# A two-layer hybrid decoder trunk on one core: expert rows scaled after turning, pass 0 by one-hot products, choice by differences

## The chip, the cores and the metric

One core of a Trainium2 chip runs the whole kernel; the other cores are idle. The metric is the device time of one execution in microseconds. The kernel was run three times for its time, and once more under the profiler.

## The reference, cut to what matters

Two decoder layers over 512 tokens of width 1024, in float32. Each layer has three kinds of attention, one output projection, a layer norm, a mixture of 16 experts of which every token takes two, and a second layer norm. What the change touches is the stretch from the first norm to the experts:

```python
x = layer_norm(DEEPNORM_ALPHA * x + einsum('bsm,md->bsd', mix, w_out[l]), ln1_g[l], ln1_b[l])
scores = sigmoid(dot(x, w_router))
biased = (scores + router_bias).reshape(N, N_GROUPS, EXPERTS_PER_GROUP)
g_sel = argmax(sum(top_k(biased, 2)[0], axis=-1))       # one group of four experts for a token
_, local = top_k(biased[g_sel], 2)                      # two experts of that group
w = scores[expert] / sum(scores[expert])
h = silu(x @ w_gate[e]) * (x @ w_up[e]) * gate          # for the tokens of expert e
y = h @ w_down[e]
x = layer_norm(DEEPNORM_ALPHA * x + y, ln2_g[l], ln2_b[l])
```

## The kernel before, in words

**Order of the work.** The program is written as many small streams (Python generators). A planner, the class Flow (line 97), plays them against a simple model of the engines with a cost for each step, always takes the step that can start first (its start plus 0.002 us times the stream's priority number decides, so that a low number wins a tie), and emits its instructions at once. Each engine executes its own queue strictly in the order emitted; the waits between engines come from the data. The costs are the writer's: `pe(0.22, f)` books 0.22 us of TensorE.

**Layout.** Tokens lie in 4 blocks of 128 (NT), the width in 8 slices of 128 (KD). `X[:, t]` holds block t, token per partition. The 8 PSUM banks are split into two pools, ACC and PS, of four banks each in the stretch in question.

**From the projection to the choice.** `s_wout` (917) makes the output projection, its second half block by block; `s_half` (968) adds the residual and takes statistics of each half-row; `s_stat` (975) gives mean and inverse deviation, the last step on POOL. `s_router` (1022) does not wait for the norm: it turns the raw rows, multiplies them with `wg` (router weights times the norm's scale) and corrects for mean, deviation and shift afterwards on VectorE (1041, 1045, 1046). `s_norm1` (1055) uses `s_norm` (982): four VectorE steps of half a row per block (990, 998) write the normed rows into X, and a DMA on SP's queue (1060) copies them to `XD` in HBM. `s_choose` (1064), for two blocks at a time, computes the scores from exp (1070) and then the rank of each expert in its group from two comparisons, is_ge and is_gt, that are combined (1084 to 1088), the best group by a maximum (1092 to 1096), the one-hot `ohb` of the chosen experts (1098), the one-hot of each of the two choices `oh` (1104) and the end of the chosen expert's table (`eb`, 1106, 1107).

**From the choice to the rows.** Each expert has 96 slots (CAP), and 16x96 slots make 12 passes (NP) of 128 slots. `s_rank` (1177) counts on TensorE how many earlier tokens chose the same expert (1188 to 1191), picks each choice's position with `oh` (1195, 1198), moves a position beyond the end far away (1200, 1201) and splits it into pass and slot (1203 to 1212). `s_table` (1228) turns that into the list of token numbers by slot with 16 small products (1221, 1225). `s_gather` (1451) fetches for each pass the 128 rows of its slots from XD by an indirect DMA from POOL (1293) into one of three buffers. `turn_rows` (1484) turns them on TensorE (1503) and `s_rows` (1462) evacuates them, half a pass on ScalarE and half on VectorE (279, 280).

**The passes.** `s_passes` (1576) runs, for p = 0 to 11, the first products of pass p (1594: gate and up, 32 columns of slots per expert unit), the turns for pass p-1's hidden rows (1500) and for pass p+1's rows (1503), and the second products of pass p-1 (`second`, 1557, product at 1568). Pass 0 has no second products behind it. `s_act` (1468) takes silu on ScalarE and the product with it on VectorE (1472, 1473). Expert weights are loaded by `s_load_experts` (1346) on SP's queue into buffers as these come free. While TensorE has nothing to do between the projection and pass 0, `s_warm` (1117) books dummy products of ones (1124) until the first gather is due.

**After the passes.** `s_alpha` (1615) multiplies blocks 0 and 2 of X with the residual's factor on POOL or ScalarE; blocks 1 and 3 get it through a product with `ident_alpha` (1673). `s_combine` (1650) adds the experts' results. `overflow` (1369) handles experts with more than 96 tokens, behind a branch.

Of the kernel before, what the change touches and what calls it, by code (L numbers as in the profile page):

```python
# [6 lines left out]
F32 = mybir.dt.float32  # L7
# [27 lines left out]
FAR = 8192.0  # L35

# [159 lines left out]
def body(tc, sb, pp, dr, x, w_in, attn_sinks, c_q_norm_g, c_kv_norm_g, w_uq, w_ukv, w_out, ln1_g, ln1_b,  # L196
# [105 lines left out]
    ident_alpha = fixed(P)  # L302
    V.tensor_scalar(ident_alpha, ident, ALPHA, None, op0=OP.mult)
# [16 lines left out]
    desc = fixed(4)  # L320
    V.tensor_scalar(desc, iotf[:, :4], -1.0, float(NE), op0=OP.mult, op1=OP.add)
    lower = fixed(4, 4)
    G.iota(lower, pattern=[[1, 4], [-1, 4]], base=0, channel_multiplier=0, allow_small_or_imprecise_dtypes=True)
    V.tensor_scalar(lower, lower, 0.0, None, op0=OP.is_gt)
# [45 lines left out]
    for key, n in (("sg", 2 * NE), ("zz", 2 * NE), ("bi", 2 * NE), ("c1", 8 * NE), ("c2", 8 * NE), ("g4", 2 * NE), ("rk", 2 * NE), ("gs", 8), ("m1", 8),  # L370
                   ("pick", 8), ("oh", 4 * NE), ("wts", 4), ("posk", 4), ("row", 4), ("eb", 4), ("op", 4 * NP)):
        for q in range(NT // 2):
            small((key, q), n)
# [105 lines left out]
    def layer(l, xready, prev_free):  # L479
# [542 lines left out]
        def s_router(t):  # L1022
            yield E("gain")
            r0, z = smalls["r0", t], smalls["zz", t // 2][:, t % 2 * NE:(t % 2 + 1) * NE]
            for h in range(2):
# [17 lines left out]
            yield E("stat", t)  # L1043
            mv, rs = smalls["mv", t], smalls["rs", t]
            yield ve(16, lambda: V.scalar_tensor_tensor(r0, gbv[:, 0], mv[:, 0:1], r0, op0=OP.mult, op1=OP.subtract))
            e = yield ve(16, lambda: V.scalar_tensor_tensor(z, r0, rs[:, 0:1], gbv[:, 1], op0=OP.mult, op1=OP.subtract))
# [8 lines left out]
        def s_norm1(t):  # L1055
            yield E("gb1")
# [4 lines left out]
            flow.set(E("xd", t), xd)  # L1061


        def s_choose(q):
# [5 lines left out]
            t = yield ac(32, lambda: A.activation(sg, smalls["zz", q], AF.Exp), [flow.now])  # L1070
            flow.set(E("exp", q), t)
            C1, C2 = (c.rearrange("p (g a b) -> p g a b", a=4, b=4) for c in (c1, c2))
            b84, G84, R84 = (a.rearrange("p (g a) -> p g a", a=4) for a in (bi, g4, rk))
            other = b84[:, :, None, :].to_broadcast([P, 8, 4, 4])
            own = b84[:, :, :, None].to_broadcast([P, 8, 4, 4])
            gs2, pick2 = (a.rearrange("p (t g) -> p t g", t=2) for a in (gs, pick))
# [5 lines left out]
            e = yield v(lambda: V.tensor_tensor(bi2, sg2, rb[:, None, :].to_broadcast([P, 2, NE]), op=OP.add))  # L1082

            yield v(lambda: V.tensor_tensor(C1, other, own, op=OP.is_ge))
            yield v(lambda: V.tensor_tensor(C2, other, own, op=OP.is_gt), [e])
            yield v(lambda: V.tensor_tensor(C1, C1, lower[:, None, :, :].to_broadcast([P, 8, 4, 4]), op=OP.mult), [])
            yield v(lambda: V.tensor_tensor(C1, C1, C2, op=OP.max))
            yield v(lambda: V.tensor_reduce(R84, C1, axis=AX.X, op=OP.add))
# [3 lines left out]
            yield v(lambda: V.tensor_reduce(m1[:, 0:2], gs2, axis=AX.X, op=OP.max))  # L1092
            yield v(lambda: V.tensor_tensor(pick2, gs2, m1[:, 0:2, None].to_broadcast([P, 2, 4]), op=OP.is_equal))
            yield v(lambda: V.tensor_tensor(pick2, pick2, desc[:, None, :].to_broadcast([P, 2, 4]), op=OP.mult))
# [682 lines left out]
```

## Time and profile before

| what | us |
|---|---|
| median of three runs (861.07, 863.41, 863.6) | 863.41 |
| the profiled execution | 862.1 |
| its span, first to last instruction | 860.3 |
| TensorE busy in it (96%) | 821.7 |
| VectorE busy (59%) | 509.6 |
| ScalarE busy (37%) | 315.3 |

The page gives busy times of PE (TensorE), PEld (its weight loads), DVE (VectorE), ACT (ScalarE) and POOL (GpSimd), and then the groups of instructions that cost most. A timeline lists an engine's instructions in order of time: start, duration, line and operation, tiles written and read, how many alike follow one another, and in brackets how long the engine was idle before and what ended the idle time. TensorE's instructions overlap, so a duration is longer than the distance to the next start. PE busy includes the dummy products.

### The profile page before, as it was taken

Reading aid. Unit: us, or ns where it says so; the run is one execution under the profiler, and the core shown is the slowest. Engines: PE = TensorE matmul, PEld = TensorE weight load, DVE = VectorE, ACT = ScalarE, POOL = GpSimd, SP = SyncE. Lnnn points to the kernel's source line nnn. Section 1 sums busy time; section 2 is a strip of 40 time slices with the busy share of each in tenths; the row PEclk is TensorE's granted clock in tenths of the full one; section 3 lists DMA queues with packets and bytes.
Section 4 is the critical chain, followed back from the end, with each engine's and each line's share of the span. In section 5 each row is a group of like instructions: output and inputs, shape, how many; then the busy total and the mean of one; then the engine's idle time right before and its main releaser. Section 6 shows DMA issues by size and latency. Waiting matters only on the chain. (4 is left out here: it accounts for less than half of the span.)

```text
span 860.3 us, 16084 instructions
## 1 busy us (share of the span) xinstructions
PE 821.7 (96%) x6288; PEld 536.8 (62%) x6288; DVE 509.6 (59%) x1504; ACT 315.3 (37%) x790; POOL 103.8 (12%) x135
## 2 busy tenths in 40 slices
PE   7999999999999999979999999999999999999795
PEld 7878886668894333323587889766788743334232
DVE  6799999955681120002998999999458413100057
ACT  4434647963111222212145274677521012221111
POOL 1010102000111111100211001300100111110004
PEclk9999999999999999989999999999999999999898
DMA  8422430175377999976544217010946489999562
GB/s 267 142 77 86 137 134 26 28 266 181 121 252 242 350 370 376 371 266 246 182 102 141 74 50 269 2 50 29 339 147 219 146 306 371 372 372 369 192 265 98
DMA packets 119148, 172.82 MB, mean 201 GB/s; under 512 B 12102, under 2 KB 95558, under 8 KB 119057
## 3 DMA queue, kind: packets, MB, share of 16 engines
q1 hardware_dynamic: 112720, 156.12, 52.8%
q0 software_dynamic: 6336, 15.52, 5.0%
q8 instruction: 53, 0.87, 0.4%
q14 instruction: 39, 0.31, 0.1%
HBM read 154.01 MB, written 25.17 MB: 208 GB/s over the span
## 5 line engine op out<-in xcount | busy, mean ns | idle before, releaser
L283 PE MATMUL bank<-ring,ra 128*128 128x512 f32 (+4 forms) x448 | 167.1, 373 | 0.5 <-ACT fa L605 0.5
L1594 PE MATMUL bank<-fa,ra 128*32 128x512 f32 x1080 | 161.3, 599 | 1.2 <-DVE ra L280 0.7
L284 PE MATMUL bank<-ring,xl 128*128 128x512 f32 (+4 forms) x448 | 157.6, 352 | 0.9 <-DVE xl L452 0.9
L285 PE MATMUL bank<-ring,ra 128*128 128x512 f32 (+4 forms) x448 | 157.9, 353 | 0.0
L279 ACT ACTIVATE fa<-bank 128x512 f32<-128x512 f32 (+3 forms) x170 | 85.4, 516 | 155.9 <-PE bank L441 82.7
L1473 DVE TENSOR_TENSOR fa<-fa,bank 128x256 f32<-128x256 f32 x24 | 10.1, 419 | 214.6 <-ACT fa L1472 214.6
L1594 PEld LDWEIGHTS bank<-fa,ra 128*32 128x32 f32 x1080 | 50.3, 111 | 75.0 <-issue 67.6
L1568 PE MATMUL bank<-fa 128*32 128x512 f32 x504 | 83.8, 625 | 11.1 <-PEq L1376 10.0
L283 PEld LDWEIGHTS bank<-ring,ra 128*128 128x128 f32 x448 | 85.0, 190 | 14.9 <-issue 7.1
L285 PEld LDWEIGHTS bank<-ring,ra 128*128 128x128 f32 x448 | 84.8, 189 | 8.2
L284 PEld LDWEIGHTS bank<-ring,xl 128*128 128x128 f32 x448 | 85.2, 190 | 7.4 <-DVE xl L452 1.3
L441 PE MATMUL bank<-fa 128*128 128x128 f32 (+1 forms) x456 | 71.6, 281 | 7.3 <-DMA fa<-in_x_dram 5.5
L441 PEld LDWEIGHTS bank<-fa 128*128 128x128 f32 (+1 forms) x456 | 55.3, 144 | 24.1 <-issue 6.0
L474 ACT ACTIVATE ring<-fa 128x1024 fp32r<-128x1024 f32 (+4 forms) x56 | 49.4, 897 | 55.7 <-PE bank L284 52.4
L1594 PE MATMUL bank<-ring,ra 128*32 128x512 f32 x360 | 67.1, 592 | 0.0
L1472 ACT ACTIVATE fa<-bank 128x256 f32<-128x256 f32 x24 | 9.2, 384 | 153.0 <-PE bank L1594 153.0
L475 DVE TENSOR_TENSOR ring<-fa,ring 128x1024 fp32r<-128x1024 f32 (+4 forms) x56 | 57.9, 1041 | 7.5 <-ACT ring L474 7.4
L747 DVE MATCH_REPLACE8 aux<-fa,aux 128x256 f32<-128x256 f32 (+2 forms) x96 | 51.6, 540 | 0.0
L746 DVE MAX8 fa<-aux 128x8 f32<-128x256 f32 (+2 forms) x96 | 50.3, 547 | 0.1
L1568 PEld LDWEIGHTS bank<-fa 128*32 128x32 f32 x504 | 19.6, 112 | 46.7 <-issue 44.9
L787 PE MATMUL bank<-fa 64*128 64x256 f32 (+7 forms) x256 | 47.4, 413 | 0.0
L800 ACT ACTIVATE fa<-fa 128x256 f32<-128x256 f32 (+3 forms) x89 | 44.5, 503 | 0.0
(222 smaller groups left out, 1219.3 us busy)
## 6 DMA issues: line engine op xcount, KB each, us to landing
fa<-in_w_gate_dram SPq DMA_DIRECT2D x45, 512.0 KB, 9.4
fa<-in_w_up_dram SPq DMA_DIRECT2D x45, 512.0 KB, 10.4
fa<-in_w_down_dram SPq DMA_DIRECT2D x21, 1024.0 KB, 9.7
xl<-in_w_down_dram SPq DMA_DIRECT2D x9, 1024.0 KB, 11.6
fa<-in_w_out_dram SPq DMA_DIRECT2D x8, 1024.0 KB, 5.9
yd<-fa SPq DMA_DIRECT2D x16, 512.0 KB, 8.3
ring<-in_w_gate_dram SPq DMA_DIRECT2D x15, 512.0 KB, 9.0
ring<-in_w_up_dram SPq DMA_DIRECT2D x15, 512.0 KB, 8.9
```

The source lines that it names most:

```text
L279: return Step([("A", 0.05 + n / 1200, lambda: A.activation(dst, src, AF.Copy)), ("V", 0.12 + n / 960, lambda: V.tensor_copy(dst, src))], a ...
L283: T.matmul(ps, xh, wh, start=start, stop=False)
L284: T.matmul(ps, xl, wh, start=False, stop=False)
L285: T.matmul(ps, xh, wl, start=False, stop=stop)
L441: T.transpose(ps[:n, j, :], s, ident)
L474: yield Step([("A", 0.09 + n / 1200, lambda: A.activation(hv, raw, AF.Copy))], None)
L475: t = yield ve(n, lambda: V.tensor_tensor(lv, raw, hv.bitcast(F32), op=OP.subtract))
L746: yield ve(nk, lambda: V.max(m8, sc))
L747: yield ve(nk, lambda: V.match_replace(sc, m8, sc, MARK))
L787: T.matmul(got[1][:, a * nk:(a + 1) * nk], qs[h], ks[h], start=True, stop=True)
L1568: T.matmul(a[1][cs], ht[:, j, cs], E("raw", e, 2).got[1][:, j, n * 512:(n + 1) * 512], start=j == 0, stop=j == 1)
L1594: T.matmul(acc[1][cs], gh[:, 4 * u + j, cs], E("raw", e, u).got[1][:, j], start=u + j == 0, stop=u + j == 4)
```

## The change

In words: the first norm's scale and shift are no longer applied before the rows are written to HBM. `s_norm1` makes (x - mean) / deviation in one ScalarE step per block, and that is written and gathered; scale and shift come in when a pass's turned rows are evacuated, where they are a number per partition, so that each of the 8 slices has its own instruction. X itself gets scale, shift and the residual's factor in a new `s_alpha` on VectorE, four half-row steps for every block, once pass 0's rows and the table are made and the row is written. Pass 0's rows are not gathered any more: `s_first` builds, for each block, the matrix m of zeros and ones that says which token stands in which of slots 0 to 127, and multiplies X's block with it on TensorE, accumulated over the four blocks into two banks, which gives the rows turned. The choice ranks by one subtraction and one comparison with a tiny negative threshold below the diagonal instead of two comparisons combined, for experts and groups alike, and the limit of an expert's table is applied to all positions before a choice's own is picked.

```diff
 def s_router(t):
     ...
-    e = yield ve(16, lambda: V.tensor_tensor(r0, r0, gp[1][:, :NE], op=OP.add))
+    tp = e
+    es = yield E("stat", t)
+    mv, rs = smalls["mv", t], smalls["rs", t]
+    e = yield ve(16, lambda: V.scalar_tensor_tensor(r0, gbv[:, 0], mv[:, 0:1], r0, op0=OP.mult, op1=OP.subtract), [es])
+    e = yield ve(16, lambda: V.scalar_tensor_tensor(r0, r0, rs[:, 0:1], gbv[:, 1], op0=OP.mult, op1=OP.subtract), [e])
+    e = yield ve(16, lambda: V.scalar_tensor_tensor(z, gp[1][:, :NE], rs[:, 0:1], r0, op0=OP.mult, op1=OP.subtract), [e, tp])
 def s_norm1(t):
-    e = yield from s_norm(t, (aux.of(F32), gb1), E("stat", t).got, er, None, True)
+    for h in range(2):
+        yield E("seen", h, t)
+    e = yield ve(1, lambda: V.tensor_scalar(rs[:, 1:2], mv[:, 0:1], rs[:, 0:1], -1.0, op0=OP.mult, op1=OP.mult), [er])
+    e = yield ac(D, lambda: A.activation(X[:, t], X[:, t], AF.Identity, scale=rs[:, 0:1], bias=rs[:, 1:2]), [e])
+def s_alpha(t):
+    yield E("gb1")
+    yield E("first")
+    yield E("table")
+    yield E("xd", t)
+    for h in range(2):
+        yield ve(512, lambda: V.scalar_tensor_tensor(X[:, t, cs], X[:, t, cs], ALPHA, g[:, cs], op0=OP.mult, op1=OP.mult))
+        e = yield ve(512, lambda: V.scalar_tensor_tensor(X[:, t, cs], b[:, cs], ALPHA, X[:, t, cs], op0=OP.mult, op1=OP.add))
 def s_choose(q):
+    def beaten(c, vals, n, left):
+        yield v(lambda: V.tensor_tensor(c, vals[:, :, None, :].to_broadcast([P, n, 4, 4]), vals[:, :, :, None].to_broadcast([P, n, 4, 4]),
+                                        op=OP.subtract))
+        yield v(lambda: V.tensor_tensor(c, c, beats[:, None].to_broadcast([P, n, 4, 4]), op=OP.is_gt))
+        yield v(lambda: V.tensor_reduce(left, c, axis=AX.X, op=OP.add))
     ...
+    yield from beaten(C1, b84, 8, R84)
     ...
+    yield from beaten(C2, gs2, 2, pick.rearrange("p (t g) -> p t g", t=2))
+    yield v(lambda: V.scalar_tensor_tensor(G84, pick[:, :, None].to_broadcast([P, 8, 4]), 8.0, R84, op0=OP.mult, op1=OP.add))
+    e = yield v(lambda: V.tensor_scalar(ohb[:, 2 * q:2 * q + 2].rearrange("p t e -> p (t e)"), g4, 2.0, None, op0=OP.is_lt))
     ...
+    e = yield v(lambda: V.tensor_tensor(oh.rearrange("p (k e) -> p k e", k=2), g4[:, None, :].to_broadcast([P, 2, 2 * NE]),
+                                        iotf[:, :2, None].to_broadcast([P, 2, 2 * NE]), op=OP.is_equal))
 def s_warm():
-    while E("gathered").t is None or flow.free["T"] < E("gathered").t:
+    while E("warm").t is None or flow.free["T"] < E("warm").t:
+def s_first():
+    for t in range(NT):
+        yield E("posk", t // 2)
+        yield E("normed", t)
+        ...
+        yield v_small(lambda: V.tensor_scalar(m[:, t], iotf, pos[0], None, op0=OP.is_equal), [])
+        te = yield v_small(lambda: V.scalar_tensor_tensor(m[:, t], iotf, pos[1], m[:, t], op0=OP.is_equal, op1=OP.add))
+        if t == NT - 1:
+            flow.set(E("warm"), te)
+        def f():
+            for k in range(KD):
+                T.matmul(banks_[k // 4][1][:, k % 4 * P:(k % 4 + 1) * P], X[:, t, k * P:(k + 1) * P], m[:, t], start=t == 0 and k % 4 == 0,
+                         stop=t == NT - 1 and k % 4 == 3)
+        te = yield pe(0.109 * KD, f, [te])
+flow.go(B0 + 62.9, s_first())
 def s_rows(p, banks_, te):
-    for h in range(2):
-        t = yield from turned(banks_[h], banks_[h][1].rearrange("p (a b) -> p a b", b=P), te, E("gt", p).got[0][:, 4 * h:4 * h + 4])
+    for k in range(KD):
+        dst, src = E("gt", p).got[0][:, k], banks_[k // 4][1][:, k % 4 * P:(k % 4 + 1) * P]
+        g, b = gcol[:, 0, k:k + 1], gcol[:, 1, k:k + 1]
+        t = yield Step([("A", 0.22, lambda: A.activation(dst, src, AF.Identity, scale=g, bias=b)),
+                        ("V", 0.21, lambda: V.tensor_scalar(dst, src, g, b, op0=OP.mult, op1=OP.add))], [te])
 def s_passes():
-    yield from turn_rows(None, 0, GT)
+    te = yield E("first")
+    ...
+    flow.go(B0 + PRIO["experts"] - 20, s_rows(0, E("first").got, te))
-for p in range(NP):
+for p in range(1, NP):
     flow.go(B0 + PRIO["experts"], s_gather(p))
```

The old `s_alpha` on POOL or ScalarE goes, as does `ident_alpha`: the product at 1673 takes the plain identity. `s_rank` compares the positions with the limits right after the rank products, before it needs the one-hots of the choices. The overflow branch gets the same scale and shift.

## Rows read from the trace of the kernel before

**Rows 1.** The page: its first line and the busy times of the engines.

```profile
span 860.3 us, 16084 instructions
...
PE 821.7 (96%) x6288; PEld 536.8 (62%) x6288; DVE 509.6 (59%) x1504; ACT 315.3 (37%) x790; POOL 103.8 (12%) x135
```

**Rows 2.** Busy time by stretch: PE, PEld, DVE, ACT, POOL, then PE clock, DMA share, GB/s.

```profile
239.40:260.90 21.50, 20.44 (x351) 19.71 (x350) 15.16 (x84) 2.96 (x6) 3.79 (x4) 1.00 0.68 236
...
660.20:681.90 21.70, 20.38 (x351) 19.64 (x349) 15.16 (x83) 2.95 (x6) 3.66 (x4) 1.00 0.66 229
```

**Rows 3.** Timeline of PE, first layer: start us, us, engine, line, operation, tiles.

```profile
239.38 1.74 PE L1124 MATMUL bank<-ones 128*128 128x128 bf16 x28
240.96 0.61 PE L441 MATMUL bank<-fa 128*128 128x128 f32 x4
...
242.31 1.06 PE L1035 MATMUL bank<-fa 128*128 128x16 f32 x8 [0.17 <-ACT fa L279]
...
250.17 0.17 PE L1191 MATMUL bank<-ohb,before 128*128 128x16 bf16 x1 [0.25 <-DVE ohb L1098]
...
253.22 0.69 PE L1221 MATMUL bank<-rv,sl 128*128 128x24 bf16 x16
...
259.56 1.10 PE L1503 MATMUL bank<-fa 128*128 128x128 f32 x8 [0.39 <-DMA fa<-xd,ti]
260.90 7.16 PE L1594 MATMUL bank<-fa,ra 128*32 128x512 f32 x64 [0.25 <-ACT ra L279]
267.99 1.09 PE L1503 MATMUL bank<-fa 128*128 128x128 f32 x8
```

**Rows 4.** Timeline of DVE in the same stretch.

```profile
241.24 0.14 DVE L1098 SCALAR_TENSOR_TENSOR ohb<-fa 128x32 bf16<-128x32 f32 x1
...
243.41 0.17 DVE L1041 TENSOR_TENSOR fa<-fa,bank 128x16 f32<-128x16 f32 x1 [0.53 <-PE bank L1035]
...
244.44 0.23 DVE L1046 SCALAR_TENSOR_TENSOR fa<-fa 128x16 f32<-128x16 f32 x1
...
244.72 0.74 DVE L998 SCALAR_TENSOR_TENSOR fa<-fa 128x512 f32<-128x512 f32 x1
245.38 0.17 DVE L1080 TENSOR_SCALAR fa<-fa 128x32 f32<-128x32 f32 x1
...
246.20 0.28 DVE L1084 TENSOR_TENSOR fa<-fa 128x128 f32<-128x128 f32 x1
...
249.94 0.18 DVE L1098 SCALAR_TENSOR_TENSOR ohb<-fa 128x32 bf16<-128x32 f32 x1
...
250.75 0.21 DVE L1195 TENSOR_TENSOR fa<-fa,bank 128x64 f32<-128x64 f32 x1
250.99 0.22 DVE L1198 TENSOR_REDUCE fa<-fa 128x4 f32<-128x64 f32 x1
...
251.44 0.16 DVE L1201 SCALAR_TENSOR_TENSOR fa<-fa 128x4 f32<-128x4 f32 x1
...
253.95 0.18 DVE L1225 TENSOR_SCALAR ti<-bank 128x24 int32<-128x24 f32 x1 [0.41 <-PE bank L1221]
```

**Rows 5.** Timeline of ACT in the same stretch.

```profile
244.70 0.23 ACT L1070 ACTIVATE fa<-fa 128x32 f32<-128x32 f32 x1 [2.45 <-DVE fa L1046]
...
268.16 0.38 ACT L1472 ACTIVATE fa<-bank 128x256 f32<-128x256 f32 x1 [6.36 <-PE bank L1594]
```

**Rows 6.** Timeline of POOL in the same stretch.

```profile
255.02 1.26 POOL L1293 DMA_INDIRECT fa<-xd,ti  x1 [12.88 <-DVE fa L1144]
...
257.89 0.99 POOL L1293 DMA_INDIRECT fa<-xd,ti  x1 [0.31 <-issue]
```

**Rows 7.** The page's costliest groups: busy us, mean ns, idle before and its releaser.

```profile
L1594 PE MATMUL bank<-fa,ra 128*32 128x512 f32 x1080 | 161.3, 599 | 1.2 <-DVE ra L280 0.7
```

**Rows 8.** Timeline of SP's queue, first layer.

```profile
264.60 0.37 SPq L1355 DMA_DIRECT2D fa<-in_w_gate_dram  x1
```

**Rows 9.** Busy time by stretch, columns as in group 2, middle of the experts' stage.

```profile
300.00:320.00 20.00, 20.00 (x184) 7.83 (x188) 6.55 (x16) 6.11 (x11) 4.04 (x4) 1.00 1.07 372
```

More of the change, by code (lines that the diff above doesn't have):

```diff
@@ L35 @@
 FAR = 8192.0
+TINY = 1.5e-38
+NONE = 4096.0
 class Event:
@@ L1069, in s_choose @@
             sg2, bi2 = (a.rearrange("p (t e) -> p t e", t=2) for a in (sg, bi))
-            t = yield ac(32, lambda: A.activation(sg, smalls["zz", q], AF.Exp), [flow.now])
+            t = yield ac(32, lambda: A.activation(sg, smalls["zz", q], AF.Exp, scale=-1.0), [flow.now])
             flow.set(E("exp", q), t)
-            C1, C2 = (c.rearrange("p (g a b) -> p g a b", a=4, b=4) for c in (c1, c2))
+            C1 = c1.rearrange("p (g a b) -> p g a b", a=4, b=4)
+            C2 = c2[:, :2 * NE].rearrange("p (t a b) -> p t a b", a=4, b=4)
@@ L1073, in s_choose @@
             b84, G84, R84 = (a.rearrange("p (g a) -> p g a", a=4) for a in (bi, g4, rk))
-            other = b84[:, :, None, :].to_broadcast([P, 8, 4, 4])
-            own = b84[:, :, :, None].to_broadcast([P, 8, 4, 4])
-            gs2, pick2 = (a.rearrange("p (t g) -> p t g", t=2) for a in (gs, pick))
+            gs2 = gs.rearrange("p (t g) -> p t g", t=2)
             def v(fn, after=None):
                 return ve(60, fn, after)
+            def beaten(c, vals, n, left):
[3 more added lines that the diff above has]
+                yield v(lambda: V.tensor_reduce(left, c, axis=AX.X, op=OP.add))
@@ L1180, in s_rank @@
                 yield E("ohb", s)
-            oh, c1, c2, posk, row, eb, op = (smalls[k, q] for k in ("oh", "c1", "c2", "posk", "row", "eb", "op"))
+            oh, c1, c2, posk, row, op = (smalls[k, q] for k in ("oh", "c1", "c2", "posk", "row", "op"))
             gp = yield Take(PS)
@@ L1213, in s_rank @@
             flow.set(E("rank", q), e)
+        def s_first():
+            for t in range(NT):
+                yield E("posk", t // 2)
+                yield E("normed", t)
+                if t == 0:
+                    gm = yield Take(WT)
+                    m = rshape(gm[1], NT, P)
+                    banks_ = yield Take(PS, 2)
+                pos = [smalls["posk", t // 2][:, 2 * k + t % 2:2 * k + t % 2 + 1] for k in range(2)]
+                yield v_small(lambda: V.tensor_scalar(m[:, t], iotf, pos[0], None, op0=OP.is_equal), [])
[7 more added lines that the diff above has]
+                te = yield pe(0.109 * KD, f, [te])
+            WT.put(gm, te)
+            E("first").got = banks_
+            flow.set(E("first"), te)
+        flow.go(B0 + 62.9, s_first())
         def v_small(fn, after=None):
@@ L1397, in overflow @@
                                 T.transpose(pb[:, j], g[:, (4 * b + j) * P:(4 * b + j + 1) * P], ident)
-                            A.copy(gt[:, 4 * b:4 * b + 4], pb)
+                            for j in range(4):
+                                A.activation(gt[:, 4 * b + j], pb[:, j], AF.Identity, scale=gcol[:, 0, 4 * b + j:4 * b + j + 1],
+                                             bias=gcol[:, 1, 4 * b + j:4 * b + j + 1])
                         for u in range(2):
@@ L1613, in layer @@
         nxt = [Event() for _ in range(NT)]
-        def s_alpha(t):
-            yield E("gu", 2 * t)
-            yield Step([("G", 2.2, lambda: G.tensor_scalar(X[:, t], X[:, t], ALPHA, None, op0=OP.mult)),
-                        ("A", 1.0, lambda: A.activation(X[:, t], X[:, t], AF.Copy, scale=ALPHA))], None)
-            flow.set(E("alpha", t), flow.free["G"])
         def s_far(t):
```

83 lines of the change are left out of this document (33 added, 50 removed).

## The prediction

> **What bounds the kernel now.** I read the page's head first: TensorE (PE) is the busiest engine, so time is won only where PE has nothing useful to do [rows 1]. The table by stretches, cut where the output projection ends and where the experts begin, shows such a place in each layer: 21.5 us in the first, 21.7 us in the second [rows 2]. PE counts as busy there, but PE's timeline shows what it does: dummy products of ones (L1124) from 239.38 on, two small pieces of the router, two rank products, the table's product (L1221), and nothing of weight until the rows of pass 0 are turned at 259.56 and its first product starts at 260.90 [rows 3]. So each stretch is a chain that PE waits out, and the other timelines give its links: last half-row off the projection, router product at 242.31, its logits finished at 244.67 (L1046), exp on ScalarE, the choice on VectorE (DVE) up to the one-hot at 250.12 (L1098), rank, table written at 254.13 (L1225), gather issued at 255.02, rows seen by PE at 259.56, turned and evacuated by 260.90 [rows 3 to 6]. The second layer repeats it, so one layer is worked out and doubled. Of what follows, passes run back to back: the main group of L1594 idles 1.2 us in 1080 instructions and never for a DMA [rows 7].
>
> **The change, part by part** (times of the first layer, as in the rows; the last projection product ends at 239.4).
>
> *Products of blocks 0 and 1.* Pass 0 now comes from 4 blocks of 8 fp32 products of 128 columns. In the router's row 4 fp32 products of 16 columns are 8 instructions in 1.06 us; 8 turns of 128 columns, one instruction each, take 1.09 [rows 3]. So a product is two instructions, and a block is 16 of them: twice those times less one tail that both rows contain, 1.8 us; the planner books 0.87. Lower bound 1.1 (one instruction each, as turns), upper 2.2. Blocks 0 and 1 belong to tokens whose choice is over early: their one-hot stands at 241.24 now [rows 4], and with eight half-rows of the norm (0.7 each) gone from in front of it and three steps fewer it should come some 5 us sooner, so that with rank and m these two are ready about when the projection ends. Placed at 239.4 they fill PE to 243.0 and the last router turns move from 240.96 to 243.0, 2.0 us late; placed after the router product they cost nothing, since only dummies stand there; slipped in before the projection's end they cost up to 3.6. I take **+1.6**, near the middle case, because the planner orders by readiness and believes them half as long; ends 0 and 3.6.
>
> *Router and norm.* Scale and shift leave the chain: three small steps on DVE after the product become one, the others done ahead. Now the sum comes at 243.41 and the logits end at 244.67, with a half-row of the norm between; afterwards one step of 0.23 at 243.41 ends them at 243.64 [rows 4]. **-1.0**. The norm itself becomes one ScalarE pass instead of four DVE half-rows of about 0.7; it stands beside the choice, and ScalarE has only 0.23 of exp to do there [rows 5].
>
> *Choice.* Exp ends at 244.93, but DVE is in L998 until 245.4; then 16 steps to the one-hot, among which a half-row and the rank of the other pair are mixed, end at 250.12: 5.2 us [rows 4, 5]. New: 13 steps with an empty engine. Dependent small steps start 0.24 apart (250.75, 250.99), 0.03 more than the first lasts; a 128-wide one lasts 0.28, so 0.32, and I take the reciprocal as one of these [rows 4]. 9x0.24+4x0.32 = 3.4, with the hand-over from ScalarE 3.6. **-1.6** with the wait for L998 gone. The four steps that made the one-hots and limits behind it become one, beside PE's rank products.
>
> *Rank.* After the one-hot, PE takes about 0.4, then four steps give the position: 1.35 against 1.48 up to L1201's end at 251.60. **-0.1** [rows 3, 4].
>
> *Pass 0 without table and gather.* Now 9.3 us run from 251.60 to 260.90. New: two 128-wide steps per block, 0.6 with their gap; then blocks 2 and 3, 3.6; the table's product and the count behind it, which are ready by then (2.5 us of steps, plus 0.8 for the ones mixed in), stand in PE's order before pass 0 and cost 0.65 (their row is 0.69 with its tail) [rows 3, 4]. The evacuations in eighths start as each part is done and feed a product that takes 0.9 us per part; only the first can show, 0.1. Together 4.9: **-4.4**.
>
> Sum: 1.6-1.0-1.6-0.1-4.4 = -5.5 in the first layer, and -5.8 in the second, whose wait for the gather is 0.2 to 0.3 longer now [rows 2]: **-11.3**.
>
> *What moves off the path.* Rows now go to HBM unscaled, once the norm is done, some 5 us earlier; the SP queue stands free meanwhile: its next weight load, at 264.60, waits for pass 0 (L1594), so loads shift with PE [rows 8]. The gather of pass 1 takes the place of that of pass 0: 5.4 us from table to PE (254.13 to 259.56). Pass 0 starts 0.1 before the table is written and lasts 7.1, so this gather has 1.4 us to spare [rows 3, 6]. Evacuating each pass's rows in eighths: a 256-wide one takes 0.38 on ScalarE, so I estimate 0.28 for 128, four per engine, 1.1 against 0.6; from pass 2 on 3.6 us of second products hide it; without them, at pass 1, the first eighth alone must be there. Price 0, at most 0.5 per layer. Sixteen DVE half-rows of scale and shift, 11 us a layer, stand in passes 0 and 1, when DVE has nothing else on the path: the first silu product is wanted only after pass 1. Behind the table in DVE's queue they wait for the row writes, long landed. Price 0. The end of a layer keeps its work.
>
> One rule speaks against this placing. While DVE worked, the gather at 255.02 took 1.26 against 0.99 for one issued with DVE idle, so the row shows 0.27 us of disturbance at most [rows 6]. By the Trainium skill, "SBUF — State Buffer", section "Who interferes with whom", a DVE instruction with two SBUF inputs contends with a GpSimd instruction that reads SBUF, and whichever issues first holds the shared port for its whole length. The steps of scale and shift have two SBUF inputs. By the row the sum keeps the gather hidden; by the rule, if the gather loses only one turn, it does too, and if it loses all of them, the third rival below follows.
>
> The sum stands against the profiled execution, 862.1 us around a span of 860.3 [rows 1]: 862.1-11.3 = 850.8. The median of the runs is 863.4 (861.07 to 863.6), 1.3 higher; I write 851.
>
> **Rivals.** (1) *Blocks 0 and 1 cost nothing*, because PE meets them only after the router product, where only dummies stand now. For it: that gap, from 243.4 to 250.17 [rows 3]. Against: they are ready sooner and outrank the dummies. 2x1.6 less: 847.6; with one-instruction products 2x1.4 less again: 845. (2) *The gain is given back to the weights.* In the middle of the experts' stage DMA runs full, 372 GB/s [rows 9]; were a load already just in time there, PE would wait for it and end where it does now: 862. Against: the loads are released by PE's own progress [rows 8] and PE never waited for one [rows 7]; the only new load is that two gathers fall beside the first weights, 1 MB or 2.8 us of that rate, at a point that is not full yet. (3) *The gather is late, and the kernel slower.* On POOL the gather of pass 1 stands beside the eleven us of half-rows on DVE. If it gets the port only behind them, it is issued near 11.5 us after pass 0 starts and lands 4.5 later, at 16, where PE wants it at 7.1: 9 us idle per layer against 5.6 won, 2x3.4 more: 869. It decides for slower once the gather is more than 7 us late; up to 1.4 late it is not seen. (4) *The change reaches less*: both blocks fall wholly on the path and a pass-1 evacuation shows, 2x2.5 back: 856.
>
> **How the numbers follow.** The forecast and its neighbourhood (848 to 854) 0.55; rival 1 0.20; rival 4 0.13; rival 2 0.07; rival 3 0.05. The range takes the first three but for the outer part of 1 and 4: 845.5 to 857.5. A measurement tells about 0.3%, 2.6 us, from no change: faster 0.88, same 0.07, slower 0.05.
>
> **What would show it.** From the last projection product to the first L1594-type product: 16 us in place of 21.5, split as above: the logits one step behind the router product; 3.6 us from exp to the one-hot; 64 new PE instructions in four blocks of 1.8 us, two after the position, two near 239 to 243; the table's product just before pass 0; no gather for pass 0, and PE seeing the gather of pass 1 without an idle. Wrong would be a block of 0.9 us (one instruction per product), the router's turns not delayed, an idle of PE for a gather at pass 1, or PE waiting for weights in the middle of the stage.

## The result: 854.2 us, and the profile after

Six runs of the changed kernel have the median 854.16 us (853.28 to 857.44), six of the kernel before 863.37 (861.07 to 863.96): a ratio of 0.9899, with a 95% interval of 0.9881 to 0.9917. It is faster, by 9.2 us. The forecast's terms add up to 11.3; 851 lies 12.4 below that median only because they were taken off the profiled execution of 862.1. The page of the profiled execution (854.43 us) begins:

```profile
span 852.6 us, 15795 instructions
...
PE 814.9 (96%) x6072; PEld 527.8 (62%) x6072; DVE 538.8 (63%) x1586; ACT 339.1 (40%) x854; POOL 100.3 (12%) x133
```

The span is 7.7 us shorter than in [rows 1]. VectorE and ScalarE have more to do, PE 216 instructions less: dummy products gone, blocks of the one-hot product come. The two stretches of [rows 2], cut again at the end of the projection and at the first product of pass 0 (columns as there):

```profile
239.40:256.95 17.55, 17.18 (x233) 16.70 (x233) 11.80 (x55) 3.92 (x7) 0.55 (x1) 1.00 0.64 227
657.00:673.65 16.65, 16.43 (x230) 15.95 (x228) 10.89 (x50) 3.92 (x7) 0.55 (x1) 1.00 0.61 220
```

(The second is cut about 1 us late at its left end: the projection ends near 655.95, and cut there the stretch is 17.7 us long.) PE's timeline in the first layer, against [rows 3]:

```profile
239.55 3.84 PE L1243 MATMUL bank<-fa 128*128 128x128 f32 x32 [0.29 <-DVE fa L1237]
243.22 1.06 PE L1133 MATMUL bank<-ones 128*128 128x128 bf16 x16
244.12 0.60 PE L440 MATMUL bank<-fa 128*128 128x128 f32 x4
...
245.46 1.06 PE L1034 MATMUL bank<-fa 128*128 128x16 f32 x8
...
250.54 0.17 PE L1200 MATMUL bank<-ohb,before 128*128 128x16 bf16 x1
...
252.56 3.84 PE L1243 MATMUL bank<-fa 128*128 128x128 f32 x32
256.23 0.55 PE L1257 MATMUL bank<-rv,sl 128*128 128x24 bf16 x16
...
256.95 3.65 PE L1641 MATMUL bank<-fa,ra 128*32 128x512 f32 x32
...
264.30 1.09 PE L1547 MATMUL bank<-fa 128*128 128x128 f32 x8
```

and VectorE's, against [rows 4]:

```profile
237.87 0.18 DVE L1204 TENSOR_TENSOR fa<-bank,fa 128x32 f32<-128x32 f32 x1
...
241.19 0.25 DVE L1223 TENSOR_TENSOR rv<-fa 128x96 bf16<-128x96 f32 x1
241.36 0.68 DVE L969 SCALAR_TENSOR_TENSOR fa<-fa,bank 128x512 f32<-128x512 f32 x1
...
246.62 0.23 DVE L1045 SCALAR_TENSOR_TENSOR fa<-bank,fa 128x16 f32<-128x16 f32 x1 [2.40 <-ACT fa L1062]
...
250.30 0.18 DVE L1112 TENSOR_SCALAR ohb<-fa 128x32 bf16<-128x32 f32 x1
...
251.57 0.22 DVE L1211 TENSOR_REDUCE fa<-fa 128x4 f32<-128x64 f32 x1
...
258.10 0.17 DVE L1261 TENSOR_SCALAR ti<-bank 128x24 int32<-128x24 f32 x1
```

In the kernel before, VectorE came to the last half-row of the residual earlier:

```profile
239.58 0.69 DVE L970 SCALAR_TENSOR_TENSOR fa<-fa,bank 128x512 f32<-128x512 f32 x1
```

The reader is to see the chain shrink behind the router product and stretch ahead of it. Step by step, in us of the first layer (exp starts at 246.89 on ScalarE, 244.70 before [rows 5]):

| step | before | after | difference | forecast |
|---|---|---|---|---|
| last turns for the router start | 240.96 | 244.12 | +3.16 | +1.6 |
| router product to logits | 242.31 to 244.67 | 245.46 to 246.85 | -0.97 | -1.0 |
| exp to one-hot | 244.70 to 250.12 | 246.89 to 250.48 | -1.83 | -1.6 |
| one-hot to position | to 251.60 | to 251.79 | -0.17 | -0.1 |
| position to pass 0 | to 260.90 | to 256.95 | -4.14 | -4.4 |
| pass 0 starts | 260.90 | 256.95 | -3.95 | -5.5 |

Four terms came within 0.3 us; one is 1.6 off. In the second layer pass 0 starts at 673.65 instead of 681.91 [rows 2], a further 4.3 us gained.

The gather of pass 1, the subject of the third rival, on POOL:

```profile
259.16 1.26 POOL L1329 DMA_INDIRECT fa<-xd,ti  x1 [15.33 <-DVE fa L1153]
260.72 1.00 POOL L1329 DMA_INDIRECT fa<-xd,ti  x1 [0.31 <-issue]
262.03 0.99 POOL L1329 DMA_INDIRECT fa<-xd,ti  x1 [0.30 <-issue]
```

These are the gathers of passes 1 to 3. They went out though VectorE was at the half-rows of scale and shift from 259.55 on, and the turns of pass 1 at 264.30 show no idle time.

### The profile page after: what moved, and what is told of

It reads as the page before. It is cut to its first block, busy times and chain, and to the rows that moved or that the text cites. A ratio compares the mean times of both kernels' runs of the same rounds, so it can differ in the third digit from the quotient of the medians.

```text
span 852.6 us, 15795 instructions
## 1 busy us (share of the span) xinstructions
PE 814.9 (96%) x6072; PEld 527.8 (62%) x6072; DVE 538.8 (63%) x1586; ACT 339.1 (40%) x854; POOL 100.3 (12%) x133
## 5 line engine op out<-in xcount | busy, mean ns | idle before, releaser
L1641 PE MATMUL bank<-fa,ra 128*32 128x512 f32 x1080 | 160.5, 595 | 0.2
L281 ACT ACTIVATE fa<-bank 128x256 f32<-128x256 f32 (+3 forms) x172 | 86.1, 515 | 131.0 <-PE bank L440 87.4
L1641 PEld LDWEIGHTS bank<-fa,ra 128*32 128x32 f32 x1080 | 47.8, 111 | 78.4 <-issue 65.9
L1641 PE MATMUL bank<-ring,ra 128*32 128x512 f32 x360 | 67.1, 592 | 0.0
L1507 DVE TENSOR_SCALAR ra<-bank,fa 128x128 f32<-128x128 f32 x108 | 41.0, 408 | 26.7 <-ACT ra L1506 23.9
L1506 ACT ACTIVATE ra<-bank,fa 128x128 f32<-128x128 f32 x84 | 34.6, 458 | 44.3 <-DVE ra L1507 40.6
```

What stands on the lines that cost most here:

```text
L281: return Step([("A", 0.05 + n / 1200, lambda: A.activation(dst, src, AF.Copy)), ("V", 0.12 + n / 960, lambda: V.tensor_copy(dst, src))], a ...
L1507: ("V", 0.21, lambda: V.tensor_scalar(dst, src, g, b, op0=OP.mult, op1=OP.add))], [te])
L1641: T.matmul(acc[1][cs], gh[:, 4 * u + j, cs], E("raw", e, u).got[1][:, j], start=u + j == 0, stop=u + j == 4)
```

## Experiments

The experiments ran in three groups, each with the kernel before beside it (medians 862.29, 861.68 and 862.64). Ratios are to the kernel before of the same group; those three medians and the 863.37 above differ by up to 1.7 us for the same kernel, so times of different groups can be told apart no better than that. To compare first layers whose starts differ by some tenths, I count from the router product of the third block, a row such as [rows 3] shows for the last, to the first product of pass 0: 23.80 us in the kernel before (from 237.10), 20.23 in the changed one (from 236.72). A gain there counts in both layers. The two starting rows, before and after:

```profile
237.10 0.96 PE L1035 MATMUL bank<-fa 128*128 128x16 f32 x8
```

```profile
236.72 0.96 PE L1034 MATMUL bank<-fa 128*128 128x16 f32 x8
```

So 0.38 us of the first layer's 3.95 lie ahead of this stretch, which is 3.57 shorter (3.85 in the second layer). Counted from the same row, the last router turns are 3.54 us later than before (7.40 instead of 3.86), not 3.16.

### What delays the router: PE's queue, VectorE's queue, or both

Two things stand ahead of the last router turns now. On PE the products of blocks 0 and 1 (32 instructions) hold 239.55 to 243.22. On VectorE the last half-row of the residual (L969), which makes the rows that are to be turned, starts at 241.36, behind position, m, sl and rv of the first pair (L1204 to L1223); before it started at 239.58. The edits move one or both, and the planner then orders the rest anew.

**Blocks 0 and 1 behind the router product.**

```diff
+                if t == 0:
+                    yield E("logits", NT - 1)
                 te = yield pe(0.109 * KD, f, [te])
```

> Only the products of blocks 0 and 1 on PE move: they wait in the planner for the last block's logits; the position and m steps on DVE stay where they are. In the changed kernel the last router turns start at 244.12 us (240.96 before). Theory P (the two blocks on PE, 3.7 us in front of the turns, are what delays them): the turns start near 241, 3 us sooner in each layer, about 848. Theory D (the rank and m steps in front of the last half-row on DVE, which starts at 241.36 in place of 239.58, are what delays them): the turns start no sooner than 242.7, 1.4 us per layer, about 851.5. If the blocks then stand between logits and rank products and delay these, nothing is won: 854.

852.76 (851.05 to 853.55), ratio 0.9881 (0.9854 to 0.9909); 19.45 from the third router product. The half-row now starts at 239.33 and the turns come at 241.37, behind 44 dummies. Yet pass 0 gains 0.8 a layer only, since a new wait takes the place of the old one:

```profile
243.85 3.79 PE L1243 MATMUL bank<-fa 128*128 128x128 f32 x32
247.47 2.17 PE L1133 MATMUL bank<-ones 128*128 128x128 bf16 x36
249.48 0.17 PE L1197 MATMUL bank<-start_row,ones 128*128 128x16 bf16 x1
```

The one-hot is done at 248.00, and PE starts the rank products at 249.48. The planner books a block at 0.87 us and it takes 1.83, so it believes PE free nearly 2 us before it is, fills that time with dummies, and the dummies stand in the queue behind the blocks.

**The first pair's rank behind the last logits**, which takes its steps out of VectorE's way, and the blocks with them:

```diff
             for s in range(2 * q + 2):
                 yield E("ohb", s)
+            if q == 0:
+                yield E("logits", NT - 1)
```

> The whole rank of the first two blocks, with it their m steps and their products, waits for the last block's logits, so that neither DVE nor PE has any of it in front of the last half-row and the last router turns. P and D together: turns back near 241 in the first layer, 3.2 us per layer, about 848. If the steps moved now stand between the steps of the choice and slow it (some 18 steps of 0.1 to 0.3 us), 1 to 2 us per layer come back: 850 to 852.

850.53 (849.79 to 851.82), ratio 0.9858 (0.9833 to 0.9883); 19.02. The half-row starts at 239.47 and the turns at 240.62, as before the change; blocks (245.15 to 248.8) and dummies again hold the rank products, which start at 249.50 for a one-hot of 247.93.

**Only the tail of the first pair's rank behind the half-row**: what follows the position (the pass, sl, rv) waits, blocks 0 and 1 stay.

```diff
             flow.set(E("posk", q), e)
+            if q == 0:
+                yield E("half", 1, NT - 1)
```

> Only DVE's queue changes: the steps that follow the first pair's positions (pass and slot, hot columns) wait for the last half-row; positions, m and the two blocks of products keep their place. Theory D: the last half-row starts near 240 and the turns at 241, about 848.5. Theory P: block 0 still stands in front of the turns and block 1 in front of the router's product, so the router's product comes only about 1.4 us sooner per layer, about 851.5.

850.35 (849.99 to 851.78), ratio 0.9862 (0.9835 to 0.9888); 18.78. With the half-row early, PE takes block 0, then the turns at 241.44, then block 1, and the router product comes at 243.67 instead of 245.46. Each theory is half right: the half-row is early, as D says, and the blocks still stand in the way, as P says.

**The true price of a block alone:**

```diff
-                te = yield pe(0.109 * KD, f, [te])
+                te = yield pe(0.229 * KD, f, [te])
```

> Only the planner's price of a block changes, 0.229 us per product in place of 0.109, about what the traces show (1.83 us for 8). The blocks stay where they are, but the dummy products behind them go. Theory: of the 3.2 us by which the last router turns were late, 0.9 were 16 dummies emitted because the planner believed PE free; the turns then start at the end of the blocks, 0.9 us sooner in each layer: 852.4. If the turns wait for DVE instead (last half-row at 241.36, statistics until 242.8), nothing changes: 854.

853.74 (851.69 to 854.29), ratio 0.99 (0.9882 to 0.9919): not to be told from the changed kernel. The trace shows 19.33: the dummies at 243.22 are gone and the turns come at 243.47, but blocks and half-row stay where they are.

**Blocks late, tail late and the true price together** (the first, third and fourth diff):

> Three edits at once: the products of blocks 0 and 1 behind the last logits (as in e1_blocks_late), the DVE steps after the first pair's positions behind the last half-row (as in e3_tail_late), and the blocks' price 0.229. In e1_blocks_late the one-hot of the last pair was written at 248.0 and its rank products started at 249.5, behind 36 dummies that followed blocks booked at half their length. Theory (order of the two queues is all that was lost): the rank products follow the one-hot within 0.3 us, and the turns start near 241; from the last projection product to pass 0 about 15 us in place of 17.7, 2.7 us per layer, about 848.5. Rival (the moved steps slow the choice by as much): 850.5, like e2_rank_late.

848.41 (847.35 to 849.52), ratio 0.985 (0.9832 to 0.9868), and 16.78 from the third router product:

```profile
240.10 0.61 PE L440 MATMUL bank<-fa 128*128 128x128 f32 x4
...
241.45 1.06 PE L1034 MATMUL bank<-fa 128*128 128x16 f32 x8
...
242.81 3.79 PE L1245 MATMUL bank<-fa 128*128 128x128 f32 x32
...
246.74 0.17 PE L1200 MATMUL bank<-ohb,before 128*128 128x16 bf16 x1
...
253.15 3.65 PE L1645 MATMUL bank<-fa,ra 128*32 128x512 f32 x32
```

The turns are no later than before the change, the blocks lie where dummies lay, and the rank product starts as the one-hot ends (246.68). This is the fastest version with all of the computation, 5.8 us below the changed kernel by the medians, 6.8 by the two profiled executions, and 4.1 if each is taken from the kernel before of its own group (13.3 and 9.2 below it). The stretch is 7.02 us shorter than before, and the forecast without its +1.6 for the blocks makes 7.1. So the order of two queues, with the price that helped to set it, accounts for the whole miss in the stretch. No part alone brought more than 1.5 of the 3.45 that all three bring in the first layer (20.23 to 16.78).

### What the product and the choice are worth by themselves

**Pass 0 gathered as before**, the rest of the change kept:

```diff
-        flow.go(B0 + 62.9, s_first())
...
-            te = yield E("first")
...
+            yield from turn_rows(None, 0, GT)
...
-        for p in range(1, NP):
+        for p in range(NP):
             flow.go(B0 + PRIO["experts"], s_gather(p))
```

> The change without its product: pass 0's rows are gathered and turned as before, everything else (norm on ScalarE, rows scaled after turning, choice by differences) stays. From the position to pass 0 it needs the old 9.3 us in place of 5.2, but the turns are not delayed by the blocks (3.2 us minus what DVE's order costs, 0 to 1.8). Theory (the product gains 4.1 us behind the position and loses 1.4 to 3.2 in front of it): 1 to 2.7 us per layer slower than with it, 856 to 859.5. Rival (the product is where the gain is, the rest gives nothing): 862.

The half-rows of scale and shift then wait for the table and the written row alone, and dummies run until the first gather is due.

861.94 (859.98 to 864.97, ten runs), ratio 1.0001 (0.9987 to 1.0014): nothing is left, the number of the rival. Yet pass 0 is reached in 22.71 us instead of 23.80, and in the second layer in 22.46 (from 656.14 to 678.60) instead of 24.09. Less than the 2.7 per layer of the forecast's choice and router terms, because the last turns again start late, at 242.37 behind 44 dummies, and the gathers take longer: 5.3 us from issue to landing in the middle where they took 4.6. But a gain of 2.7 in all must show somewhere. By the second layer's pass 0 the trace is 3.3 ahead (678.60 against 681.91), and it ends 0.4 behind. Of these 3.7 us, 3.3 are lost in one place, at the branch for overflowing experts, where PE idles some 5 us and the granted clock falls. The stretch after it in slices of 3 us (columns as in [rows 2]), first of the kernel before, then of this one:

```profile
798.70:801.70 3.00, 1.47 (x8) 0.46 (x12) 0.00 (x0) 0.00 (x0) 0.00 (x0) 0.50 0.65 205
801.70:804.70 3.00, 3.00 (x20) 0.90 (x16) 0.00 (x0) 0.60 (x1) 0.00 (x0) 0.50 0.09 29
804.70:807.70 3.00, 3.00 (x35) 0.91 (x28) 0.00 (x0) 0.00 (x0) 0.98 (x1) 1.00 0.22 35
```

```profile
795.30:798.30 3.00, 0.79 (x1) 0.13 (x1) 0.00 (x0) 0.00 (x0) 0.00 (x0) 0.50 0.69 228
798.30:801.30 3.00, 1.22 (x9) 0.32 (x12) 0.00 (x0) 0.00 (x0) 0.00 (x0) 0.50 0.06 19
801.30:804.30 3.00, 3.00 (x20) 0.64 (x16) 0.00 (x0) 0.28 (x1) 0.00 (x0) 0.50 0.02 5
804.30:807.30 3.00, 3.00 (x28) 0.79 (x24) 0.00 (x0) 0.31 (x1) 0.97 (x1) 0.83 0.53 168
```

At 0.50, the lower level of 1.2 GHz, the products take twice as long: in the kernel before the 16 second products ahead of the branch are one row of 1.93 us, the 16 behind it one of 3.64. In this kernel the low clock holds a slice longer, and PE idles 6.8 us in two pieces where it idled 4.8 (first the kernel before, then this one):

```profile
793.50 1.93 PE L1568 MATMUL bank<-fa 128*32 128x512 f32 x16
800.23 3.64 PE L1568 MATMUL bank<-fa 128*32 128x512 f32 x16 [4.80 <-PEq L1376]
```

```profile
797.51 1.03 PE L1610 MATMUL bank<-fa 128*32 128x512 f32 x1 [5.04 <-PEq L1410]
800.32 2.78 PE L1610 MATMUL bank<-fa 128*32 128x512 f32 x12 [1.78 <-issue]
```

The last two turns of rows in that layer stand 22.2 us apart (789.58 to 811.79) against 18.9; over the kernels of this study that have the branch the distance goes from 17.9 to 22.2. The next three kernels take the branch out to test this.

**The kernel before, the changed kernel and the one with pass 0 gathered, each without the branch.** The treatment of experts with more than 96 tokens is left out.

```diff
-            e = yield pe(0.5, overflow, [max(flow.free.values())])
+            e = yield pe(0.5, lambda: None, [max(flow.free.values())])
```

> The kernel before without the branch for experts with more than 96 tokens (that treatment is left out). In its trace TensorE idles 4.8 to 5.2 us behind the branch in each layer and runs at a granted clock of 0.50 for about 7 us after it. Both theories: with the branch gone the last two turns of rows stand 12 to 13 us apart in place of 18.9 and 19.8, so some 13 us are won, 848 to 850. It is the base of the two runs beside it.

> The changed kernel without the branch (the treatment of experts with more than 96 tokens is left out). Theory: the change's worth lies in the stretch before pass 0 alone, 4.0 and 4.3 us in the two layers, so it stands 8 to 9 us below the kernel before without the branch. Rival: part of the 9.2 us measured with the branch came from the branch's stretch; then the difference here is under 7.

> The changed kernel with pass 0 gathered as before, without the branch (the treatment of experts with more than 96 tokens is left out). With the branch it took 861.9 against 861.7 for the kernel before, although its trace reaches pass 0 earlier by 1.1 and 1.6 us. Theory: the branch's stretch gave that back (22.2 us between the last two turns of the second layer where the kernel before has 18.9), so without the branch it stands 2 to 3.5 us below the kernel before without the branch. Rival: it is given back elsewhere, by its gathers among the half-rows of scale and shift (one took 4.3 us), and the difference here is under 1.

| without the branch | median | runs | ratio to the kernel before | third router product to pass 0, by layer |
|---|---|---|---|---|
| kernel before | 846.07 | 845.16 to 846.87 | 0.9815 (0.9781 to 0.9849) | 23.98, 23.99 |
| changed kernel | 838.78 | 838.66 to 839.46 | 0.9733 (0.97 to 0.9766) | 20.23, 20.23 |
| pass 0 gathered | 843.08 | 842.2 to 844.31 | 0.9778 (0.9744 to 0.9811) | 22.79, 22.56 |

With pass 0 gathered it is now 3.0 us below its base, so the branch's stretch had taken the gain back. The product of pass 0 is worth 4.3 us by this (843.08 less 838.78), the rest of the change 3.0. The changed kernel stands 7.3 below, between the two theories' numbers, and that is what its stretch shows: twice 3.75. Of the 9.2 measured with the branch, nearly 2 therefore aren't to be found in the stretch that was changed; they are of the size of what the branch scatters. The two profiled executions were 7.7 apart, and the kernel before itself had medians from 861.68 to 863.37 from one group to the next. The branch costs 16.6 us (862.64 less 846.07), more than the 13 I expected, and most of the scatter with it: seven runs of the kernel before lay over 5.2 us in that group, four without the branch over 1.7. The rows of granted clock on the two pages of the kernel before, with and without the branch:

```profile
PEclk9999999999999999989999999999999999999898
```

```profile
PEclk9999999999999999999999999999999999999998
```

**The change with the old choice**, 16 steps on an otherwise free VectorE (the old lines of `s_choose` up to the one-hots of the two choices):

```diff
-            yield from beaten(C1, b84, 8, R84)
+            yield v(lambda: V.tensor_tensor(C1, other, own, op=OP.is_ge))
+            yield v(lambda: V.tensor_tensor(C2, other, own, op=OP.is_gt), [e])
...
-            yield from beaten(C2, gs2, 2, pick.rearrange("p (t g) -> p t g", t=2))
+            yield v(lambda: V.tensor_reduce(m1[:, 0:2], gs2, axis=AX.X, op=OP.max))
...
```

> The change with the old choice (two comparisons combined, maximum of the groups, 16 steps to the one-hot, two to the one-hots of the choices): three more dependent steps of 0.22 to 0.33 on DVE in front of the one-hot of the last pair, 0.7 to 0.9 us, and one more behind it, beside PE. Theory (of the 1.8 us that exp to one-hot got shorter, only this part is the choice's own, the rest is DVE freed of the norm): 0.7 to 1.0 us per layer, about 856. Rival (all of it is the choice): 857.8.

857.67 (856.87 to 858.53), ratio 0.9951 (0.9934 to 0.9968), 3.5 above the changed kernel (5.2 if each is taken from the kernel before of its own group), which is the rival's number. From exp to the one-hot the old steps take 4.10 us (247.18 to 251.28) where the new take 3.59 and the kernel before took 5.42. So of the 1.83 won there 1.3 came from VectorE's freedom and 0.5 from fewer steps. The trace is nearer the theory: 20.83 against 20.23 to pass 0 makes 1.2 in two layers; the trace puts another 2.4 behind the second layer's next to last pass (13.0 and 20.9 us between turns against 12.4 and 19.1), at the branch and beside it, where the choice has no part.

### The evacuations in eighths

Each pass's eight evacuations were to go in parallel, four per engine, 1.1 us. In the changed kernel they take turns wherever both engines work on one pass (pass 1's eight all fell to ScalarE). Pass 0's begin so:

```profile
255.54 0.41 DVE L1507 TENSOR_SCALAR ra<-bank,fa 128x128 f32<-128x128 f32 x1 [1.09 <-PE bank L1243]
```

```profile
255.99 0.46 ACT L1506 ACTIVATE ra<-bank,fa 128x128 f32<-128x128 f32 x1 [7.36 <-DVE ra L1507]
```

The waits:

```profile
PE bank L1612 <- PEq L1412: 11.2, 2, 5.6
```

```profile
ACT ra L1506 <- DVE ra L1507: 40.6, 42, 7.4
DVE ra L1507 <- ACT ra L1506: 23.9, 43, 0.6
```

The first line is PE's greatest wait in the view of waits (us in total, times, longest), the branch again; the other two are from the same view over all engines. ScalarE waits for VectorE 42 times and VectorE for ScalarE 43 times, and pass 0's eight take from 255.54 to 258.67, 3.1 us. Each engine's next eighth lies in the bank the other is reading. The trial gives each engine one bank:

```diff
-                t = yield Step([("A", 0.22, lambda: A.activation(dst, src, AF.Identity, scale=g, bias=b)),
-                                ("V", 0.21, lambda: V.tensor_scalar(dst, src, g, b, op0=OP.mult, op1=OP.add))], [te])
+                alts = [("A", 0.36, lambda: A.activation(dst, src, AF.Identity, scale=g, bias=b)),
+                        ("V", 0.33, lambda: V.tensor_scalar(dst, src, g, b, op0=OP.mult, op1=OP.add))]
+                t = yield Step(alts[k // 4:k // 4 + 1], [te])
```

> Each pass's rows: slices 0 to 3 (one bank) are evacuated by ScalarE alone and 4 to 7 (the other bank) by VectorE alone, in place of a planner's choice for each slice. In the changed kernel the two engines wait for each other on these (ScalarE 40.6 us in 42 waits, VectorE 23.9 in 43), and the eight of pass 0 take 3.1 us. Theory: two engines on one bank are put in order, so that the waits vanish, the eight of pass 0 take about 1.6 us, and the table's write, which stands behind them on DVE (258.10), comes 1 us sooner; the time stays within 1 us of 854.2, since the first eighth is there when PE wants it and the others keep ahead. Rival: they are put in order by the tile that they write; then the waits stay. Second rival: the late eighths cost PE time somewhere; then 851 or less.

855.65 (854.09 to 858.16), ratio 0.9929 (0.9904 to 0.9953). The waits across are gone, though both engines still write one tile: in a later pass ScalarE works from 321.64 to 323.14 and VectorE from 322.07 to 323.44. So it was the bank and not the tile. The four on ScalarE run in 1.50 us, the four on VectorE in 1.36, and the table's step starts at 256.56 instead of 258.10:

```profile
255.27 1.50 ACT L1506 ACTIVATE ra<-bank,fa 128x128 f32<-128x128 f32 x4 [6.90 <-PE bank L1243]
```

```profile
257.05 1.36 DVE L1507 TENSOR_SCALAR ra<-bank,fa 128x128 f32<-128x128 f32 x4
```

But the eight of pass 0 still take 3.1 us (255.27 to 258.41, where 1.6 were expected), since VectorE's four now stand behind the table's step in its queue; it is this order that brought the table forward. Pass 0 starts 20.31 after the third router product, as with turns taken (20.23), and the time is no better. So no run here shows a gain from ending the turns.

**Both queues in order** (the kernel of 848.41) **and the banks split:**

> The kernel with both queues in order (blocks 0 and 1 after the router product at their true length, and the first pair's tail after the last half-row; 848.4 us), and the evacuations of a pass's rows split so that ScalarE has one bank and VectorE the other. Theory: the two engines no longer take turns at a bank, so the table and the gather of pass 1 come 1.5 us sooner, which nobody waits for: 848 within 1. Rival: the eighths are on the path of pass 0 after all, 0.5 to 1.5 per layer: 846.

849.8 (847.86 to 851.23), ratio 0.9856 (0.9818 to 0.9893): no gain over 848.4 (ratio 0.985). Pass 0 starts at 16.87, as in the kernel without the split (16.78); at pass 1 PE now waits for VectorE's half of the evacuation, which stands among its half-rows:

```profile
265.73 3.86 PE L1646 MATMUL bank<-fa,ra 128*32 128x512 f32 x32 [0.56 <-DVE ra L1511]
```

## Why the prediction was right, and where it was not

**Direction and mechanism.** The chain that PE waits out became shorter, by the steps that were named. The router's logits end one step behind the product (-0.97 for -1.0). The choice took 3.36 us from the end of exp for 3.6 (3.59 from its start). The rank was 0.17 shorter for 0.1. Position to pass 0 took 5.16 for 4.9: four dummies between the table's product and pass 0 (0.31 us) and the steps ahead of block 2 (0.77 for 0.6) cost more, the table's product (0.41 for 0.65) less. A block of eight fp32 products is 16 instructions in 1.83 us, for 1.8. The median lies inside the range, in which 854.16 is just above the forecast's own neighbourhood (848 to 854). Part of that is luck: the stretch gave 3.57 and 3.85 us where 11.3 in two layers were forecast, and without the branch the whole change is worth 7.3; the other 1.9 of the measured 9.2 come from no part of the change that was found.

**The mis-sized term** is "Products of blocks 0 and 1": "I take +1.6, near the middle case, because the planner orders by readiness and believes them half as long; ends 0 and 3.6". It measured +3.16 by the clock of the two traces and +3.54 from the third router product, at its upper end. Two things were wrong in it. The placing I called the middle case, start at 239.4 and turns at 243.0, is what PE did: the blocks end at 243.22, 2.26 later than the old start of the turns, and I took less than that because the planner believes them short. That belief worked the other way: over too soon in the plan, the blocks got 16 dummies behind them, 0.90 us up to 244.12. And I looked at PE's queue alone. On VectorE the same early readiness put 3.5 us of the first pair's steps ahead of the last half-row, so that the rows to be turned were finished at 242.04 only; even without the blocks the turns could not have started before that. Most of rival 4's condition, both blocks on the path, is thus what came about (856 by its sum, with an evacuation that did not show).

**Rival 1** (blocks 0 and 1 cost nothing, 847.6) did not happen, but its price was right: in the kernel that puts them behind the router product, with VectorE's queue in order too, the two stretches are 14.3 us shorter than before, for 14.5 by the rival's sum. It took 848.41, 13.3 below the kernel before of its group.

**Rival 2** (given back to the weights) did not happen. L1641 idles 0.2 us in 1080 instructions, and the first layer's passes take as long as before, from the first product of pass 0 to the first of the combination behind them (260.90 to 411.62 before, 256.95 to 407.56 after).

**Rival 3** (late gather) did not happen to the gather of pass 1: 1.26, 1.00 and 0.99 us for the first three, and no idle time on PE. "Pass 0 starts 0.1 before the table is written" became 1.3 before it (256.95 against 258.27, the end of L1261), because eighths stand ahead of it on VectorE. That used most of the time to spare, which the forecast puts at 1.4 and its own numbers at 1.6 (7.1 less 0.1 and 5.4). The rule weighed there, in the Trainium skill's "SBUF — State Buffer", "Who interferes with whom", says that the side that comes second is held for the whole of the other's instruction; none of the changed kernel's first three gathers was held for as much as a half-row (0.27 us at most against 0.69), but the fourth gather of other kernels was held through several (below).

**Eighths at price 0** held, with a duration that did not: 3.1 us instead of 1.1, from turns taken at a bank. The Trainium skill has the rule, in "PSUM — Partial Sum Buffer", section "PSUM bank collisions raise a hardware error": two engines must not touch one bank in the same partitions at once, reads included, and a dependency between them is the guard. The trace agrees: 85 waits of one engine for the other, none left when the banks are split.

**The second layer** was to give 0.3 more than the first. In the profile with the branch it did, by 0.28 (3.85 against 3.57), and for the reason given: there PE's wait for the gather before was 0.67 us in the second layer and 0.39 in the first. Without the branch the kernel before needs the same time in both layers (23.98 and 23.99), and both give 3.75. So the 0.3 is not a property of the second layer.

**What stays open**: why behind the branch PE idles 4.8 us and the low clock holds for some 6 in one kernel, and 6.8 and 9 in another, was not tried, nor whether the branch can be had without PE's idle time.

## What to carry to other kernels

When work becomes ready earlier, look in every queue for what it now stands ahead of: here it passed the last half-row on VectorE and the router's turns on TensorE, and 3.2 to 3.5 us of a gain of 7 were lost in each layer. A planner's price that is half of the truth does harm in the filling put behind the step (16 dummies, 0.90 us, here). And read a change's worth from its own stretch: a branch elsewhere in the program moved the total by as much as the effects looked for.

## What was not expected of the hardware

A gather seems to be held by VectorE's half-rows, but not always. In the kernel with pass 0 gathered the fourth gather took 3.87 us in the first layer and 4.27 in the second, and ended within 0.15 us of the last half-row:

```profile
260.39 3.87 POOL L1327 DMA_INDIRECT fa<-xd,ti  x1 [2.75 <-PE bank L1545]
...
678.76 4.27 POOL L1327 DMA_INDIRECT fa<-xd,ti  x1 [2.35 <-PE bank L1545]
```

```profile
263.44 0.69 DVE L1076 SCALAR_TENSOR_TENSOR fa<-fa 128x512 f32<-128x512 f32 x1
...
682.20 0.69 DVE L1076 SCALAR_TENSOR_TENSOR fa<-fa 128x512 f32<-128x512 f32 x1
```

With the banks split and both queues in order it took 3.70, from 261.59 until VectorE, between two half-rows, came at 265.28 to an evacuation from PSUM; with the banks split alone 3.69, up to such an evacuation at 268.84. A product with one input in PSUM, at 264.34 in the former, had not let it go. In the changed kernel the fourth gather went out in 1.09 us (265.67) amid the same half-rows, and without the branch the kernel with pass 0 gathered had 1.43 and 1.03 where it had 3.87 and 4.27. So something like the third rival's mechanism is there, at about 3 us a time, in variants of this kernel, where it struck a gather that nobody waits for until two passes later. That VectorE's steps are the cause is read from these ends that coincide; no run took the steps away, and what decides whether a gather is held, no run here shows.
